# Conformer convolution: taps on VectorE summed in PSUM, 2.5 of 8 channel tiles and the weights' low parts on GpSimd

## The chip, the cores and the metric

One core of one Trainium2 chip runs the whole program. The engines are called PE (TensorE, matmuls; PEld is its weight load), DVE (VectorE), ACT (ScalarE), POOL (GpSimd) and SP (SyncE, which issues the DMAs). The metric is the device time of one execution in microseconds; a lower one is better. "Span" is the time from the first to the last instruction of the profiled execution.

## The reference, cut to what matters

The program is one step of a decoder trunk with two layers, for a prompt of 512 positions and a sample group of 8 sequences with one position each; both share the weights and are handled as 520 columns. Layer 0 has an S5 and an HGRN2 mixer, layer 1 has the Conformer convolution module. Each layer ends with cross-attention into 256 memory tokens and a gated MLP. The part at stake is the mixer of layer 1:

```
z = h @ w_conf_in                      # 1024 -> 2048
a, gate = split(z); u = a * sigmoid(gate)
c[t] = b + sum over 31 taps j of w[j] * ext[t + j]     # per channel, causal; ext = 30 past values, then u
y = silu(layer_norm(c over the 1024 channels)) @ w_conf_out
```

For the prompt the 30 past values are zeros, so tap d (d positions back) touches the columns d to 511 only. For a sample sequence the past values come from a state, and only tap 0 touches the new position.

## The kernel before, in words

Everything is held with channels on the 128 partitions and the 520 columns along the free dimension; 1024 channels are 8 tiles (`KC`). A matmul in full precision is made of three products: activations and weights are each split into a high part of type float32r and a low part (the remainder). `load_w` (L179 to L195) does this for weights: a DMA of 512 KB into `wraw`, a copy by ACT into `whi`, and a subtraction into `wlo` on DVE or, where the caller says so, on POOL, in two halves of 128x512. `mm` (L197) then issues 8 x 3 x 2 = 48 matmuls for one tile of 128 output channels and 520 columns. PSUM tiles come from two pools: `pa` has three buffers of 1024 columns (two banks), `pb` two of 512 (one bank).

The mixer of layer 1 is `mixer1` (L1049 to L1172). `project_first` (L209) computes the first three projection tiles while the norm in front of them is finished. Then, tile by tile, PE makes the gate's and the value's projection (`pcg`, `pca`), and `gate` (L1058) turns them into `u`: DVE multiplies the gate by the norm's factor, ACT takes the sigmoid, DVE multiplies the value by the factor and by the gate.

`conv` (L1069) forms the 31 taps of one tile. ACT writes tap 0 with the bias into `cc`; DVE adds the sample's history `hs`, which `conv_history` (L1454) summed earlier, to the 8 last columns. The other 30 taps go one of three ways:

- DVE: one instruction per tap, c = u * w + c, all in SBUF (L1085). Tiles 1, 3, 6, 7 have 30 such taps, tile 5 has 16.
- POOL: ACT writes u * w into `ct` (three buffers), POOL adds it to `cc` (L1082, L1083). Tiles 0, 2, 4 (`POOL_TAPS`).
- PE: 14 taps of tile 5 (`PE_TAPS`) as matmuls with diagonal matrices (`conv_pe`, L1091), which ACT builds from the identity, and which are summed in a `pb` buffer `pcv`; DVE adds them at the end (L1087).

After the convolution come the keys of layer 1 from the memory tokens (`memory_k`, L1227: 8 tiles, two to a `pb` buffer, evacuated by ACT and DVE as `kf`, `Kh`, `Kl`), four of eight parts of the values (`memory_v`, `pvv`), and the column sums over channels for the LayerNorm (`column_sums`, L228: ones-matmuls over all eight `cc`, into `pcs`). The sums need the finished `cc` of every tile. Then follow the centring (`cmu`), the squares, a second column sum, the scaling, silu, and the output projection.

The order in which each engine takes its instructions is not the written one: the program is built under a planner that simulates the engines' time and places an instruction when its inputs are ready in that simulation (`TileContext(nc, schedule_with_timeline_sim=True)`, L1670). At run time each engine then follows its list in order. `tc.issue_after` pins a few of them, among them the value parts behind the column sums (L1140).

Of the kernel before, what the change touches and what calls it, by code (L numbers as in the profile page):

```python
# [18 lines left out]
P = 128  # L19
# [22 lines left out]
CPAIR = (1, 3)  # L42
CACT = (0, 1, 2, 3, 4, 5, 6, 7)
NE = "VG"
LG = ((0, 0, 0), (0, 0, 0), (0, 1, 1))
POOL_TAPS = {0: 30, 2: 30, 4: 30}
PE_TAPS = {5: 14}
FILL = (4, 6, 5)
# [54 lines left out]
def trunk(ctx, tc, I, O, dbg=None):  # L103
# [47 lines left out]
    def f32(t):  # L151
        return t.bitcast(F32)
# [255 lines left out]

    # ------------------------------------------------------------ S5 and HGRN2 layer
    def mixer0(nxt):  # L410
# [635 lines left out]

    # ------------------------------------------------------------ conformer layer

    def mixer1(bd, nxt, kvp, hs, mem):  # L1049
        nrm, xs = bd.nrm, bd.nrm.xs  # L1050
        l = 1
        with ExitStack() as es:
            cf = es.enter_context(tc.tile_pool(name="cf", bufs=1))
            cw = par[:, PC_CW:PC_CW + CW * KC].rearrange("p (c j) -> p c j", j=CW)

            us, cs = [], []

            def gate(n, pg, pu):  # L1058
                g = slab("cg")
                tt(V, g, pg, r, MUL)  # L1060
                act(g, g, AF.Sigmoid)
                u = slab("cu")
                tt(V, u, pu, r, MUL)
                tt(V, u, u, g, MUL)
                nc.sync.dma_start(O["p_conf"][:, n, :], u[:, LP - (CW - 1):LP])
                nc.sync.dma_start(O["s_conf"][:, n, CW - 2, :], u[:, LP:])
                us.append(u)

            def conv(n):  # L1069
                u = us[n]  # L1070
                c = cf.tile([P, NT], F32, tag="cc", name="cc", bufs=KC)
                cs.append(c)
                if n in CACT:
                    act(c, u, AF.Identity, scale=cw[:, n, CW - 1:CW], bias=pcol(PC_CB, n))
                else:
                    ts(V, c, u, cw[:, n, CW - 1:CW], pcol(PC_CB, n), MUL, ADD)
                tt(V, c[:, LP:], c[:, LP:], hs[:, n, :], ADD)
                for d in range(1, CW - PE_TAPS.get(n, 0)):
                    w = cw[:, n, CW - 1 - d:CW - d]
                    if d > CW - 1 - PE_TAPS.get(n, 0) - POOL_TAPS.get(n, 0):  # L1080
                        t = cf.tile([P, LP], F32, tag="ct", name="ct", bufs=3)
                        act(t[:, d:], u[:, 0:LP - d], AF.Copy, scale=w)  # L1082
                        tt(G, c[:, d:LP], c[:, d:LP], t[:, d:], ADD)  # L1083
                    else:
                        stt(c[:, d:LP], u[:, 0:LP - d], w, c[:, d:LP], MUL, ADD)  # L1085
                if n in part:
                    tt(V, c[:, :LP], c[:, :LP], part[n], ADD)  # L1087

            part = {}

            def conv_pe(n):  # L1091
                nt = PE_TAPS[n]
                u = us[n]
                wh = cf.tile([P, nt], F32R, tag="cwh", name="cwh", bufs=2)
                wl_ = cf.tile([P, nt], F32, tag="cwl", name="cwl", bufs=2)
                act(wh, cw[:, n, :nt], AF.Copy)
                tt(V, wl_, cw[:, n, :nt], f32(wh), SUB)
                uh, ul = (cf.tile([P, CW - 1 + LP], F32R, tag=t, name=t, bufs=1) for t in ("uh", "ul"))
                for t in (uh, ul):
                    G.memset(f32(t[:, :CW - 1]), 0.0)  # L1100
                act(uh[:, CW - 1:], u[:, :LP], AF.Copy)
                tt(V, ul[:, CW - 1:], u[:, :LP], f32(uh[:, CW - 1:]), SUB)
                ps = part[n] = pb("pcv")
                for j0 in range(0, nt, 4):
                    m = min(4, nt - j0)
                    dh = wpool.tile([P, 4, P], F32R, tag="whi", name="dh", bufs=6)
                    dl = wpool.tile([P, 4, P], F32R, tag="wlo", name="dl", bufs=6)
                    for j in range(m):
                        act(dh[:, j], ident, AF.Copy, scale=f32(wh[:, j0 + j:j0 + j + 1]))
                        act(dl[:, j], ident, AF.Copy, scale=wl_[:, j0 + j:j0 + j + 1])  # L1110
                    for j in range(m):
                        o = slice(j0 + j, j0 + j + LP)
                        for i, (a, b) in enumerate(((dh, uh), (dh, ul), (dl, uh))):
                            T.matmul(ps, a[:, j], b[:, o], start=j0 + j == 0 and i == 0,
                                     stop=j0 + j == nt - 1 and i == 2)

            wl = lambda n: load_w(I["w_conf_in"][n])
            p0 = project_first(xs, bd.ws, RC, nrm, CUTC)
            r = nrm.r
            gate(0, *p0[:2])  # L1120
            conv(0)
            for n in range(1, KC):
                pg = p0[2] if n == 1 else mm(pa("pcg"), wl(KC + n), xs)
                pu = mm(pa("pca"), wl(n), xs)
                gate(n, pg, pu)
                if n < 5:
                    conv(n)
            for n in PE_TAPS:
                conv_pe(n)
            for n in range(5, KC):  # L1130
                conv(n)
            kmem = memory_k(1, mem, kvp)
# [40 lines left out]

    # ------------------------------------------------------------ memory keys and values
    mrs = []
# [51 lines left out]
    def memory_k(l, m, kvp):  # L1227
        Kh, Kl = (kvp.tile([P, KC, NM], F32R, tag=t, name=t) for t in ("Kh", "Kl"))
        for n0 in range(0, KC, 2):
            ps = pb("pkk")  # L1230
            for n in (n0, n0 + 1):
                o = ps[:, (n - n0) * NM:(n - n0 + 1) * NM]
                if l == 1:
                    w = raw_w(I["w_xk"][l, n])
                    for k in range(KC):
                        T.matmul(o, w[:, k], m[k], start=k == 0, stop=k == KC - 1)
                else:
                    wh, wl = load_w(I["w_xk"][l, n])
                    for k, (mh, ml) in enumerate(m):
                        for i, (a, b) in enumerate(((wh, mh), (wh, ml), (wl, mh))):  # L1240
                            T.matmul(o, a[k], b, start=k == 0 and i == 0, stop=k == KC - 1 and i == 2)
            kf = slab("kf", n=2 * NM)
            ks = slice(n0, n0 + 2)
            kv = kf.rearrange("p (n m) -> p n m", n=2)
            act(kf, ps, AF.Copy)
            act(Kh[:, ks], kv, AF.Copy)
            tt(V, Kl[:, ks], kv, f32(Kh[:, ks]), SUB)
            nc.sync.dma_start(O["mem_k"][l, :, ks, :], kv)
        return Kh, Kl
# [30 lines left out]

    # ------------------------------------------------------------ cross attention
    def attention(bd, l, kv, ap, nxt, spare=None):
# [169 lines left out]

    # ------------------------------------------------------------ gated MLP with a depthwise convolution
    def conv_history(pool, hs):  # L1454
# [247 lines left out]
```

## Time and profile before

| | before |
|---|---|
| time, median of 3 runs | 1826.97 us (1825.53 to 1831.73) |
| profiled execution: span | 1828.6 us |
| PE, DVE, ACT, POOL busy | 1662.2, 1063.4, 824.8, 718.5 us |
| mean granted clock of TensorE | 0.947 |

The time of the profiled execution is given as its span; what lies around the span is not listed apart. A busy share is a mean over the whole program, in which PE is the busiest engine. Stages differ: in the Conformer convolution, which lies at about 970 to 1220 us of the span, the shares are others, and they are read from windows of the trace.

### The profile page before, as it was taken

How to read it: one execution, taken by the hardware profiler on the slowest of the kernel's cores; microseconds unless marked ns; L12 is line 12 of the kernel's file. 1: busy time of each engine (PE TensorE's matmuls, PEld its weight loads, DVE VectorE, ACT ScalarE, POOL GpSimd, SP SyncE). 2: the span in 40 equal slices, each digit the busy share in tenths (PEclk: the TensorE clock that was granted, in tenths of full speed). 3: DMA queues.
4: the chain of work that ended last, by engine and by line, in shares of the span. 5: the costliest groups of instructions: out<-in, count | busy, mean ns of one | idle time of the engine just before them, and what ended most of it. 6: DMA issues, size and time to landing. Idle time of an engine off the chain costs nothing. (4 is left out here: it accounts for less than half of the span.)

```text
span 1828.6 us, 32823 instructions
## 1 busy us (share of the span) xinstructions
PE 1662.2 (91%) x13050; PEld 1568.3 (86%) x13050; DVE 1063.4 (58%) x1869; ACT 824.8 (45%) x1637; POOL 718.5 (39%) x682
## 2 busy tenths in 40 slices
PE   8987899899898999999999775598989899999996
PEld 8987867898698999999999764388869799999996
DVE  8667486873548423333379998967353842333345
ACT  6424435672456343233356554386245533323343
POOL 2444040511027435252435769514102733525343
PEclk9978799999998999999999887799999999999998
DMA  7332321375631242323222202241672223232331
GB/s 238 101 84 69 108 69 50 119 234 185 233 129 58 87 124 90 104 76 106 80 90 69 61 27 96 74 162 47 196 242 76 70 83 102 82 104 76 110 87 56
DMA packets 81393, 194.76 MB, mean 107 GB/s; under 512 B 21648, under 2 KB 31320, under 8 KB 81240
## 3 DMA queue, kind: packets, MB, share of 16 engines
q1 hardware_dynamic: 81240, 192.66, 33.3%
q8 instruction: 103, 1.69, 0.4%
q14 instruction: 50, 0.41, 0.1%
HBM read 176.67 MB, written 12.47 MB: 103 GB/s over the span
## 5 line engine op out<-in xcount | busy, mean ns | idle before, releaser
L131 ACT ACTIVATE whi<-wraw 128x512 fp32r<-128x512 f32 (+2 forms) x504 | 290.6, 587 | 500.3 <-PE pfo L204 128.0
L138 POOL TENSOR_TENSOR wlo<-wraw,whi 128x512 fp32r<-128x512 f32 x182 | 243.9, 1344 | 319.1 <-ACT whi L131 317.1
L138 DVE TENSOR_TENSOR wlo<-wraw,whi 128x512 fp32r<-128x512 f32 (+2 forms) x322 | 210.2, 664 | 173.7 <-ACT whi L131 163.9
L138 POOL TENSOR_TENSOR cc<-cc,ct 128x509 f32<-128x509 f32 (+15 forms) x90 | 150.5, 1675 | 48.7 <-ACT ct L131 43.0
L141 DVE SCALAR_TENSOR_TENSOR cc<-cu,par,cc 128x511 f32<-128x511 f32 (+25 forms) x136 | 148.1, 1137 | 0.3
L204 PE MATMUL pfb<-xnh,wlo 128*128 128x256 f32 (+1 forms) x672 | 135.8, 283 | 0.0
L204 PE MATMUL pfb<-xnh,whi 128*128 128x256 f32 (+1 forms) x672 | 135.2, 282 | 0.0
L204 PE MATMUL pfb<-xnl,whi 128*128 128x256 f32 (+1 forms) x672 | 135.1, 282 | 0.0
L204 PE MATMUL pfa<-xnh,wlo 128*128 128x256 f32 (+1 forms) x640 | 129.3, 283 | 0.0
L204 PE MATMUL pfa<-xnl,whi 128*128 128x256 f32 (+1 forms) x640 | 128.7, 282 | 0.0
L204 PE MATMUL pfa<-xnh,whi 128*128 128x256 f32 (+1 forms) x640 | 128.6, 282 | 0.0
L204 PE MATMUL pfo<-hlo,whi 128*128 128x256 f32 x604 | 122.0, 282 | 0.0
L204 PE MATMUL pfo<-hhi,wlo 128*128 128x256 f32 x604 | 121.4, 282 | 0.0
L204 PE MATMUL pfo<-hhi,whi 128*128 128x256 f32 x604 | 120.8, 282 | 0.0
L204 PE MATMUL pf<-xnl,whi 128*128 128x256 f32 (+1 forms) x288 | 85.7, 308 | 20.8 <-DVE xnl L141 20.8
L204 PEld LDWEIGHTS pfb<-xnh,whi 128*128 128x128 f32 x672 | 104.2, 188 | 0.0
L204 PEld LDWEIGHTS pfb<-xnh,wlo 128*128 128x128 f32 x672 | 104.2, 189 | 0.0
L204 PEld LDWEIGHTS pfb<-xnl,whi 128*128 128x128 f32 x672 | 104.1, 188 | 0.0
L138 DVE TENSOR_TENSOR fa<-pfa,rstd 128x520 f32<-128x520 f32 x40 | 27.9, 699 | 124.7 <-PE pfa L204 124.7
L204 PEld LDWEIGHTS pfa<-xnh,whi 128*128 128x128 f32 x640 | 99.3, 188 | 0.0
L204 PEld LDWEIGHTS pfa<-xnh,wlo 128*128 128x128 f32 x640 | 99.2, 189 | 0.0
L204 PEld LDWEIGHTS pfa<-xnl,whi 128*128 128x128 f32 x640 | 99.2, 188 | 0.0
(457 smaller groups left out, 4650.9 us busy)
## 6 DMA issues: line engine op xcount, KB each, us to landing
wraw<-w_ffn_in SPq DMA_DIRECT2D x88, 512.0 KB
ck<-cK SPq DMA_DIRECT2D x32, 512.0 KB
cv<-cV SPq DMA_DIRECT2D x32, 512.0 KB
wraw<-w_ffn_out SPq DMA_DIRECT2D x32, 384.0 KB
wraw<-w_ab_in SPq DMA_DIRECT2D x20, 512.0 KB
wraw<-w_ffn_out SPq DMA_DIRECT2D x32, 320.0 KB
wraw<-w_xk SPq DMA_DIRECT2D x16, 512.0 KB
wraw<-w_xv SPq DMA_DIRECT2D x16, 512.0 KB
```

The lines of the kernel that those rows point to most:

```text
L131: A.activation(out, in_, f, **kw)
L138: e.tensor_tensor(out, a, b, op=op)
L141: V.scalar_tensor_tensor(out, in0, s, in1, op0=op0, op1=op1)
L204: T.matmul(ps[:, o:o + m], a[k], b[hv], start=first and k == 0 and i == 0, stop=last and k == n - 1 and i == 2)
```

## The change

1. DVE's taps run in PSUM: ACT writes tap 0 with the bias into a `pb` buffer `pcv`, DVE adds each tap there (u from SBUF, sum from and to PSUM), and the last DVE tap of a tile (d = 1) writes the sum into `cc`. The taps that DVE has are all of tiles 0, 2, 3, 5, 7 and 15 of tile 6.
2. POOL takes tiles 1 and 4 whole and taps 16 to 30 of tile 6 (`POOL_TAPS`); in tile 6 DVE adds its PSUM sum to POOL's sum. The history of the sample is added by POOL, not DVE.
3. The diagonal matmuls (`conv_pe`, `PE_TAPS`) go, with the blocks that ACT built for them.
4. `gate` works in place in PSUM: the gate's product and its sigmoid overwrite `pg`, and the slab `cg` goes.
5. The low parts of the 13 weight tiles that `wl` loads in this stage are made by POOL (`load_w(..., G)`), not DVE.
6. `conv` is a generator. DVE's tiles are one written sequence, of which `CSTEP` = 13 steps are written ahead of each projection tile, and the rest after the last.
7. The keys of layer 1 go to `pa` buffers, four tiles to a buffer.

```diff
@@ -40,11 +40,10 @@
 MEMN = (-1, -1, -1, -1)
 MEMG = ((0, 1, 2, 3), ())
 CPAIR = (1, 3)
-CACT = (0, 1, 2, 3, 4, 5, 6, 7)
 NE = "VG"
 LG = ((0, 0, 0), (0, 0, 0), (0, 1, 1))
-POOL_TAPS = {0: 30, 2: 30, 4: 30}
-PE_TAPS = {5: 14}
+POOL_TAPS = {1: 31, 4: 31, 6: 15}
+CSTEP = 13
 FILL = (4, 6, 5)
 START = (0, (0, 2, 0), 1, (2, 2, 0), (4, 4, 0), 2, (0, 4, 1), (4, 4, 1))
 CVP = (0, 1, 0, 1, 0, 1, 0, 1, 0, 1, 0, 1, 0, 0, 0, 1)
...
@@ -1053,82 +1052,72 @@
             cf = es.enter_context(tc.tile_pool(name="cf", bufs=1))
             cw = par[:, PC_CW:PC_CW + CW * KC].rearrange("p (c j) -> p c j", j=CW)
 
-            us, cs = [], []
+            us, cs = [], [None] * KC
 
             def gate(n, pg, pu):
-                g = slab("cg")
-                tt(V, g, pg, r, MUL)
-                act(g, g, AF.Sigmoid)
+                tt(V, pg, pg, r, MUL)
+                act(pg, pg, AF.Sigmoid)
                 u = slab("cu")
                 tt(V, u, pu, r, MUL)
-                tt(V, u, u, g, MUL)
+                tt(V, u, u, pg, MUL)
                 nc.sync.dma_start(O["p_conf"][:, n, :], u[:, LP - (CW - 1):LP])
                 nc.sync.dma_start(O["s_conf"][:, n, CW - 2, :], u[:, LP:])
                 us.append(u)
 
+            def tap(n, d):
+                return cw[:, n, CW - 1 - d:CW - d]
+
             def conv(n):
-                u = us[n]
-                c = cf.tile([P, NT], F32, tag="cc", name="cc", bufs=KC)
-                cs.append(c)
-                if n in CACT:
-                    act(c, u, AF.Identity, scale=cw[:, n, CW - 1:CW], bias=pcol(PC_CB, n))
-                else:
-                    ts(V, c, u, cw[:, n, CW - 1:CW], pcol(PC_CB, n), MUL, ADD)
-                tt(V, c[:, LP:], c[:, LP:], hs[:, n, :], ADD)
-                for d in range(1, CW - PE_TAPS.get(n, 0)):
-                    w = cw[:, n, CW - 1 - d:CW - d]
-                    if d > CW - 1 - PE_TAPS.get(n, 0) - POOL_TAPS.get(n, 0):
-                        t = cf.tile([P, LP], F32, tag="ct", name="ct", bufs=3)
-                        act(t[:, d:], u[:, 0:LP - d], AF.Copy, scale=w)
-                        tt(G, c[:, d:LP], c[:, d:LP], t[:, d:], ADD)
+                u, np_ = us[n], POOL_TAPS.get(n, 0)
+                c = cs[n] = cf.tile([P, NT], F32, tag="cc", name="cc", bufs=KC)
+                cut = CW - np_
+                act(c[:, LP:], u[:, LP:], AF.Identity, scale=tap(n, 0), bias=pcol(PC_CB, n))
+                tt(G, c[:, LP:], c[:, LP:], hs[:, n, :], ADD)
+                if np_ == CW:
+                    act(c[:, :LP], u[:, :LP], AF.Identity, scale=tap(n, 0), bias=pcol(PC_CB, n))
+                    cut = 0
+                elif np_:
+                    G.memset(c[:, :cut], 0.0)
+                    act(c[:, cut:LP], u[:, :LP - cut], AF.Copy, scale=tap(n, cut))
+                for d in range(cut + 1, CW):
+                    t = cf.tile([P, LP], F32, tag="ct", name="ct", bufs=3)
+                    act(t[:, d:], u[:, 0:LP - d], AF.Copy, scale=tap(n, d))
+                    tt(G, c[:, d:LP], c[:, d:LP], t[:, d:], ADD)
+                if cut:
+                    pc = pb("pcv")
+                    act(pc, u[:, :LP], AF.Identity, scale=tap(n, 0), bias=pcol(PC_CB, n))
+                    yield
+                    for d in range(2, cut):
+                        stt(pc[:, d:], u[:, 0:LP - d], tap(n, d), pc[:, d:], MUL, ADD)
+                        yield
+                    if np_:
+                        stt(pc[:, 1:], u[:, 0:LP - 1], tap(n, 1), pc[:, 1:], MUL, ADD)
+                        tt(V, c[:, :LP], c[:, :LP], pc, ADD)
                     else:
-                        stt(c[:, d:LP], u[:, 0:LP - d], w, c[:, d:LP], MUL, ADD)
-                if n in part:
-                    tt(V, c[:, :LP], c[:, :LP], part[n], ADD)
-
-            part = {}
-
-            def conv_pe(n):
-                nt = PE_TAPS[n]
-                u = us[n]
-                wh = cf.tile([P, nt], F32R, tag="cwh", name="cwh", bufs=2)
-                wl_ = cf.tile([P, nt], F32, tag="cwl", name="cwl", bufs=2)
-                act(wh, cw[:, n, :nt], AF.Copy)
-                tt(V, wl_, cw[:, n, :nt], f32(wh), SUB)
-                uh, ul = (cf.tile([P, CW - 1 + LP], F32R, tag=t, name=t, bufs=1) for t in ("uh", "ul"))
-                for t in (uh, ul):
-                    G.memset(f32(t[:, :CW - 1]), 0.0)
-                act(uh[:, CW - 1:], u[:, :LP], AF.Copy)
-                tt(V, ul[:, CW - 1:], u[:, :LP], f32(uh[:, CW - 1:]), SUB)
-                ps = part[n] = pb("pcv")
-                for j0 in range(0, nt, 4):
-                    m = min(4, nt - j0)
-                    dh = wpool.tile([P, 4, P], F32R, tag="whi", name="dh", bufs=6)
-                    dl = wpool.tile([P, 4, P], F32R, tag="wlo", name="dl", bufs=6)
-                    for j in range(m):
-                        act(dh[:, j], ident, AF.Copy, scale=f32(wh[:, j0 + j:j0 + j + 1]))
-                        act(dl[:, j], ident, AF.Copy, scale=wl_[:, j0 + j:j0 + j + 1])
-                    for j in range(m):
-                        o = slice(j0 + j, j0 + j + LP)
-                        for i, (a, b) in enumerate(((dh, uh), (dh, ul), (dl, uh))):
-                            T.matmul(ps, a[:, j], b[:, o], start=j0 + j == 0 and i == 0,
-                                     stop=j0 + j == nt - 1 and i == 2)
-
-            wl = lambda n: load_w(I["w_conf_in"][n])
+                        stt(c[:, 1:LP], u[:, 0:LP - 1], tap(n, 1), pc[:, 1:], MUL, ADD)
+                        act(c[:, 0:1], pc[:, 0:1], AF.Copy)
+                    yield
+
+            def chain(ns):
+                for n in ns:
+                    yield from conv(n)
+
+            wl = lambda n: load_w(I["w_conf_in"][n], G)
             p0 = project_first(xs, bd.ws, RC, nrm, CUTC)
             r = nrm.r
             gate(0, *p0[:2])
-            conv(0)
+            dve = chain(n for n in range(KC) if POOL_TAPS.get(n, 0) < CW)
             for n in range(1, KC):
+                for _ in range(CSTEP):
+                    next(dve)
                 pg = p0[2] if n == 1 else mm(pa("pcg"), wl(KC + n), xs)
                 pu = mm(pa("pca"), wl(n), xs)
                 gate(n, pg, pu)
-                if n < 5:
-                    conv(n)
-            for n in PE_TAPS:
-                conv_pe(n)
-            for n in range(5, KC):
-                conv(n)
+                if POOL_TAPS.get(n, 0) == CW:
+                    for _ in conv(n):
+                        pass
+            for _ in dve:
+                pass
             kmem = memory_k(1, mem, kvp)
             m = halves(slab("cmu"))
             rp, rs = slab("rstd"), slab("rs")
...
@@ -1226,9 +1215,10 @@
 
     def memory_k(l, m, kvp):
         Kh, Kl = (kvp.tile([P, KC, NM], F32R, tag=t, name=t) for t in ("Kh", "Kl"))
-        for n0 in range(0, KC, 2):
-            ps = pb("pkk")
-            for n in (n0, n0 + 1):
+        step = 4 if l == 1 else 2
+        for n0 in range(0, KC, step):
+            ps = pa("pkk") if l == 1 else pb("pkk")
+            for n in range(n0, n0 + step):
                 o = ps[:, (n - n0) * NM:(n - n0 + 1) * NM]
                 if l == 1:
                     w = raw_w(I["w_xk"][l, n])
...
@@ -1239,13 +1229,15 @@
                     for k, (mh, ml) in enumerate(m):
                         for i, (a, b) in enumerate(((wh, mh), (wh, ml), (wl, mh))):
                             T.matmul(o, a[k], b, start=k == 0 and i == 0, stop=k == KC - 1 and i == 2)
-            kf = slab("kf", n=2 * NM)
-            ks = slice(n0, n0 + 2)
-            kv = kf.rearrange("p (n m) -> p n m", n=2)
-            act(kf, ps, AF.Copy)
-            act(Kh[:, ks], kv, AF.Copy)
-            tt(V, Kl[:, ks], kv, f32(Kh[:, ks]), SUB)
-            nc.sync.dma_start(O["mem_k"][l, :, ks, :], kv)
+                if n % 2 == 0:
+                    continue
+                kf = slab("kf", n=2 * NM)
+                ks = slice(n - 1, n + 1)
+                kv = kf.rearrange("p (n m) -> p n m", n=2)
+                act(kf, ps[:, (n - 1 - n0) * NM:(n + 1 - n0) * NM], AF.Copy)
+                act(Kh[:, ks], kv, AF.Copy)
+                tt(V, Kl[:, ks], kv, f32(Kh[:, ks]), SUB)
+                nc.sync.dma_start(O["mem_k"][l, :, ks, :], kv)
         return Kh, Kl
 
     def memory_v(l, m, kvp, out):
```

Left out are hunks that change comment lines only.

## Rows read from the trace of the kernel before

**Rows 1.** The page: engines' busy time, clock by slice, end of the chain view

```profile
PE 1662.2 (91%) x13050; PEld 1568.3 (86%) x13050; DVE 1063.4 (58%) x1869; ACT 824.8 (45%) x1637; POOL 718.5 (39%) x682
PEclk9978799999998999999999887799999999999998
PE 27%; DVE 2%; DMA 1%; ACT 0%; issue 0%; SPq 0%; DVEq 0%; ACTq 0%
```

**Rows 2.** Windows of the convolution stage: busy us (instructions) of PE, PEld, DVE, ACT, POOL

```profile
972.00:1182.00 210.00, 145.20 (x868) 128.22 (x867) 199.03 (x200) 99.23 (x172) 150.54 (x90) 0.83 0.22 71
1098.00:1111.00 13.00, 0.00 (x0) 0.00 (x0) 12.65 (x20) 0.70 (x1) 12.92 (x2) 0.50 0.12 50
1111.00:1119.00 8.00, 0.86 (x2) 0.78 (x3) 0.00 (x0) 4.92 (x8) 7.69 (x7) 0.50 0.00 2
```

**Rows 3.** Instruction groups of DVE from 972.4 to 1182 us

```profile
L141 DVE SCALAR_TENSOR_TENSOR cc<-cu,par,cc 128x511 f32<-128x511 f32 (+25 forms) x136 | 148.1, 1137 | 0.3
L138 DVE TENSOR_TENSOR wlo<-wraw,whi 128x512 fp32r<-128x512 f32 x24 | 25.8, 1082 | 0.3 <-ACT whi L131 0.3
L138 DVE TENSOR_TENSOR cc<-cc,chs 128x8 f32<-128x8 f32 x8 | 7.5, 939 | 0.0
L138 DVE TENSOR_TENSOR Kl<-kf,Kh 128x512 fp32r<-128x512 f32 x4 | 5.8, 1439 | 8.7 <-ACT Kh L131 8.7
```

**Rows 4.** Instruction groups of POOL from 960 to 1182 us

```profile
L138 POOL TENSOR_TENSOR cc<-cc,ct 128x509 f32<-128x509 f32 (+15 forms) x90 | 150.5, 1675 | 48.7 <-ACT ct L131 43.0
```

**Rows 5.** Timeline (start, length, merged count) of POOL, then DVE, 1111 to 1128 us

```profile
1111.79 2.49 POOL L138 TENSOR_TENSOR cc<-cc,ct 128x486 f32<-128x486 f32 x2
1114.36 1.20 POOL L138 TENSOR_TENSOR cc<-cc,ct 128x484 f32<-128x484 f32 x1
1123.87 3.22 POOL L138 TENSOR_TENSOR cc<-cc,ct 128x507 f32<-128x507 f32 x2
1125.53 3.22 POOL L138 TENSOR_TENSOR cc<-cc,ct 128x506 f32<-128x506 f32 x2
1124.26 3.38 DVE L141 SCALAR_TENSOR_TENSOR cc<-cu,par,cc 128x483 f32<-128x483 f32 x2
1125.90 3.40 DVE L141 SCALAR_TENSOR_TENSOR cc<-cu,par,cc 128x505 f32<-128x505 f32 x2
```

**Rows 6.** Instructions by tile: ns min/median/max, first and last start us

```profile
L138 DVE TENSOR_TENSOR cg<-pcg,rstd x6: 683/686/686, 990.7 to 1081.2; 128x520 f32<-128x520 f32 x6
L138 DVE TENSOR_TENSOR cu<-pca,rstd x7: 685/686/700, 980.0 to 1091.4; 128x520 f32<-128x520 f32 x7
L138 DVE TENSOR_TENSOR cu<-cu,cg x8: 685/687/1443, 976.1 to 1093.9; 128x520 f32<-128x520 f32 x8
```

**Rows 7.** Timeline of DVE at its last taps: first two tiles in turn, then one

```profile
1177.41 1.97 DVE L141 SCALAR_TENSOR_TENSOR cc<-cu,par,cc 128x486 f32<-128x486 f32 x3
1178.05 1.34 DVE L141 SCALAR_TENSOR_TENSOR cc<-cu,par,cc 128x482 f32<-128x482 f32 x2
1178.68 1.46 DVE L141 SCALAR_TENSOR_TENSOR cc<-cu,par,cc 128x485 f32<-128x485 f32 x2
1179.42 1.48 DVE L141 SCALAR_TENSOR_TENSOR cc<-cu,par,cc 128x484 f32<-128x484 f32 x2
```

**Rows 8.** Instruction groups of POOL over the whole span

```profile
L138 POOL TENSOR_TENSOR wlo<-wraw,whi 128x512 fp32r<-128x512 f32 x182 | 243.9, 1344 | 319.1 <-ACT whi L131 317.1 <-PE pfb L204 1.1
L1305 POOL COPY qt<-q 128x8 f32<-128x8 f32 x16 | 5.0, 314 | 65.1 <-DVE q L138 65.1
```

**Rows 9.** Chain view (first row), then timeline of PE: start, length, what

```profile
1283.22 5.75 PE pq L204 x48
1118.14 23.72 PE L1236 MATMUL pkk<-mem,wraw 128*128 128x256 f32 x96 [30.59 <-ACT kf L131]
1141.70 3.60 PE L1265 MATMUL pvv<-wraw,mem 128*128 128x512 f32 x8
1181.71 4.16 PE L232 MATMUL pcs<-cc,cst 128*128 128x256 f32 x10 [1.68 <-DVE cc L141]
```

## The prediction

> **What bounds the kernel now.** I read the page first. TensorE (PE) is busy 91% of the span and its granted clock stands at 9 tenths in most slices; past the first few, the longest dip is in slices 23 to 26, 1006 to 1189 us [rows 1]. The chain of waits covers 27 + 2 + 1 = 30% of the span [rows 1], so it begins near 1280 us and says nothing of the convolution, which lies before that. I therefore went to the windows. From 972 to 1182 us, 210 us long, DVE is busy 199.0 us, POOL 150.5, PE 145.2 at a mean granted clock of 0.83, ACT 99.2 [rows 2]. DVE is the engine without slack. PE waits for it: the column sums of the LayerNorm end only at 1181.7 us, released by a DVE write to `cc` [rows 9]. So the stage is worth what its last tap is worth, and everything behind it (statistics, output projection, attention, MLP) moves with that tap.
>
> What fills DVE is not arithmetic alone. Its 136 taps took 148.1 us, 1137 ns each [rows 3]; undisturbed ones follow each other at 0.635 us when two tiles alternate (1177.41 to 1178.05) and at 0.74 us when one tile's taps follow each other (1178.68 to 1179.42) [rows 7]. POOL's 90 adds took 1675 ns each [rows 4], but 1.285 us while DVE was idle ((1114.36 − 1111.79)/2) [rows 2, 5]. With both busy, each runs at one instruction per 1.65 us (POOL 1123.87 to 1125.53, DVE 1124.26 to 1125.90) [rows 5]: they take turns. From 1098 to 1111 DVE got through 20 instructions and POOL through 2 [rows 2]. Which instructions take part can be read by tile: a product with two SBUF inputs (`cu<-cu,cg`) takes 685 to 1443 ns, while `cg<-pcg,rstd` and `cu<-pca,rstd`, same size, one input in PSUM, took 683 to 700 ns all 13 times, in a stretch where POOL was mostly adding [rows 6]. A tap of before reads `cu` and `cc`, both in SBUF. Undisturbed, 136 taps at 0.635 would be 86 us, so the turns cost DVE about 148 − 86 = 62 us, and its other two-SBUF instructions some more.
>
> **The change part by part.** All counts follow from the loops.
>
> *Taps on DVE.* Tiles 0, 2, 3, 5, 7 have 30 each and tile 6 has 15: 165 instead of 136. Each reads `u` from SBUF and the sum from PSUM, and writes PSUM (the last one of a tile writes `cc`). By rows 6 such a form doesn't take turns with POOL. The trace has no DVE instruction that both reads and writes PSUM. Bounds: 0.635 us (two tiles alternating, as if PSUM were SBUF) and 1.137 us (the mean of before, as if nothing were gained) [rows 3, 7]. Two PSUM buffers would let two tiles alternate, but the code writes one tile after the other, so most taps will follow their own predecessor; I take 0.72 us, near the 0.74 row with some alternation. 165 × 0.72 = 119 us; by the bounds 105 and 188.
>
> *The rest of DVE.* Three gate instructions per tile stay: 24 × 0.69 = 16.6 us [rows 6]. The 24 low parts of weights (25.8 us) and the 8 history adds (7.5 us) leave DVE [rows 3]. The four `Kl` stay (5.8 us at most), one join of tile 6 and two `Vl` come to about 2. In all 24 us. Started at 972: 972 + 24 + 119 = 1115 us.
>
> [...] Writing PSUM no row shows. [...]
>
> *POOL.* Tiles 1 and 4: 30 adds each, tile 6: 14, so 74 instead of 90; at the free pitch 74 × 1.285 = 95 us [rows 5]. New are the low parts of 13 weight tiles, 26 halves × 1.344 = 35 us [rows 8], and 8 history adds of 8 columns, at about 0.31 us (the nearest row is a copy of that size) 2.5 us [rows 8]. Together 133 us. Its adds can start when tile 1's gate runs, about 980 [rows 6], so 1113 us if it never waits; with 1.65 us per add, 1140. The cover for the low parts is that PE has room: after 980 it has 12 projection tiles × 5.75 = 69 us, then keys 8 tiles × 23.72/6 = 32 and four value parts × 3.6 = 14 [rows 9]: 1095 us. If POOL put its adds ahead of the low parts, a pair of projection tiles would cost (8 adds × 1.285 + 4 × 1.344) = 15.7 us, against 11.5 on PE; six pairs are then 25 us later, PE ends at 1120, level with the sum below, and nothing of its room is left.
>
> *ACT.* 74 scaled copies in place of 90 at about 0.7 us, and the 28 diagonal blocks go: less work than before, on an engine with 99.2 us in 210 [rows 2]; beside DVE's taps it costs nothing. A copy for POOL waits for one of three buffers, and behind it in ACT's queue stand the next weights' high parts and the gates; that was so before, when POOL's turns made each of these waits longer.
>
> *Diagonal matmuls.* The 42 that go stood just ahead of the keys, where PE then waited 30.59 us for `kf` [rows 9]: worth nothing. Keys of layer 1 move to the larger PSUM pool, since the small one now holds the sums; four tiles fill one buffer. That shares three buffers with the projection and costs little, as keys follow it. The sigmoid in place in PSUM keeps a buffer longer, through one more DVE product; PE's 20 us to DVE's end cover it.
>
> *Sum.* DVE 1115, POOL 1113, PE 1095. Three engines that end together wait for each other here and there; I add 5 us: 1120. Before it was 1181.7 [rows 9], so 61.7 us earlier. What follows is unchanged and moves along. The profiled execution has a span of 1828.6 us; 1828.6 − 61.7 = 1766.9. The median of the runs shown is 1.6 us under that span (0.1%), so 1765.3; I say 1766.
>
> **The rivals.**
> (a) *The join of tile 6.* DVE adds its PSUM sum to POOL's sum, and POOL's 14 adds for tile 6 are the last in its queue. If that add is queued ahead of tile 7's taps, up to 30 × 0.74 = 22 us of taps stand behind POOL's end at 1113 to 1118, so 1135 to 1140: 1780 to 1785. For it: tile 6 is written before tile 7. Against: the planner puts what is ready first; in rows 7 taps of two tiles alternate.
> (b) *A tap in PSUM is dearer than one in SBUF.* A wait for its own write in PSUM would come on top of 0.74. At 0.90, DVE ends at 972 + 24 + 148 + 5 = 1149: 1795. For it: no row shows a DVE write to PSUM. Against: reading PSUM is free [rows 6]. [...]
> (c) *Slower: PSUM taps still take turns with POOL.* Then 108 POOL instructions each let one tap through per 1.65 us (178 us) and 57 more follow at 0.72 (41 us): 972 + 24 + 178 + 41 = 1215, 33 us later than before: 1860. It decides from a mean tap of (1181.7 − 972 − 24)/165 = 1.126 us on; the mean of before, 1.137, lies just above that, so the change does lose if it removes no turn. Against: 13 of 13 instructions in rows 6. For it: those write SBUF and have no scalar column.
> (d) *Both engines packed without gaps*, 0.65 us a tap by full alternation: POOL's 1113 alone ends the stage: 1758.
>
> **How the numbers follow.** Forecast 0.58 (own range 1759 to 1777), (a) 0.15, (b) 0.14, (c) 0.07, (d) 0.06. 1752 to 1800 holds the forecast, (a), (d) and (b) up to 0.92 us a tap; left out are (c) and the far end of (b). A change under 0.3% (5.5 us) couldn't be told from none: it needs a tap between 1.09 and 1.16 us, 0.01. Faster 0.92, slower 0.07.
>
> **What would show it.** Taps on `pcv` at 0.65 to 0.75 us apart, with no mean above 0.8 while POOL adds; POOL's adds near 1.29 us, not 1.675; DVE and POOL both ending between 1108 and 1125; column sums released near 1120; PE at a higher granted clock from 990 to 1100. The prediction is wrong if taps come 0.85 us apart or more, if DVE stands idle before `cc<-cc,pcv` for over 10 us, or if the last key or value matmul, not a tap, releases the column sums.

## The result, and the profile after

The changed kernel took 1767.23 us (median; 1765.58 to 1769.77) against 1828.51 us for the kernel before on the same chip: a ratio of 0.967, 95% interval 0.9652 to 0.969. The forecast was 1766 us. The profiled execution has a span of 1768.0 us.

The page of the changed kernel, the lines that answer to [rows 1]:

```profile
PE 1646.6 (93%) x13008; PEld 1554.4 (88%) x13008; DVE 995.9 (56%) x1862; ACT 810.9 (46%) x1605; POOL 695.9 (39%) x699
PEclk9979798999999999999999999899999999999998
PE 28%; DVE 2%; DMA 0%; ACT 0%; issue 0%; DVEq 0%; ACTq 0%
```

Of the dip of four slices in the granted clock (slices 23 to 26 in [rows 1]) one slice at 8 tenths is left, the 26th, where the stage ends. DVE is busy 67 us less although it has 29 taps more. Windows of the changed kernel (start:end, length, then busy us and instructions of PE, PEld, DVE, ACT, POOL, granted clock, DMA share, GB/s), to be read against [rows 2]:

```profile
972.00:1122.00 150.00, 130.22 (x847) 116.11 (x846) 135.80 (x203) 87.66 (x148) 127.91 (x109) 0.94 0.32 100
1006.00:1050.00 44.00, 44.00 (x369) 44.00 (x369) 41.22 (x65) 26.59 (x46) 41.20 (x38) 1.00 0.24 75
1100.00:1120.00 20.00, 6.08 (x16) 4.66 (x17) 18.11 (x25) 4.37 (x8) 10.33 (x8) 0.59 0.01 5
```

The window that holds the stage is 150 us long in place of 210. DVE is still the engine with the least slack, but from 1006 to 1050 PE runs without a gap at a clock of 1.00 while DVE and POOL are both over 90% busy. Before, PE had nothing at all from 1098 to 1111 [rows 2]. What is left of PE's wait lies at the end: 6 busy us from 1100 to 1120.

DVE's groups, 960 to 1130 us (line, engine, operation, tiles, count | busy us, mean ns | idle before), which answer to [rows 3]:

```profile
L140 DVE SCALAR_TENSOR_TENSOR pcv<-cu,par,pcv 128x491 f32<-128x491 f32 (+19 forms) x160 | 109.5, 734 | 4.8 <-ACT pcv L130 3.4
...
L137 DVE TENSOR_TENSOR cu<-pca,rstd 128x520 f32<-128x520 f32 x7 | 4.9, 698 | 2.1 <-PE pca L203 2.1
...
L137 DVE TENSOR_TENSOR pcg<-pcg,rstd 128x520 f32<-128x520 f32 x6 | 4.2, 706 | 2.5 <-PE pcg L203 2.5
L137 DVE TENSOR_TENSOR cu<-cu,pcg 128x520 f32<-128x520 f32 x6 | 4.1, 689 | 0.0
L137 DVE TENSOR_TENSOR Kl<-kf,Kh 128x512 fp32r<-128x512 f32 x4 | 4.0, 1012 | 0.0
```

And POOL's in the same stretch, against [rows 4]:

```profile
L137 POOL TENSOR_TENSOR cc<-cc,ct 128x493 f32<-128x493 f32 (+15 forms) x74 | 94.1, 1275 | 4.9 <-ACT ct L130 1.1
L137 POOL TENSOR_TENSOR wlo<-wraw,whi 128x512 fp32r<-128x512 f32 x26 | 33.5, 1299 | 7.7 <-ACT whi L130 7.3 <-ACT cc L130 0.4
...
L137 POOL TENSOR_TENSOR cc<-cc,chs 128x8 f32<-128x8 f32 x8 | 1.6, 200 | 0.7 <-ACT cc L130 0.7
```

A tap costs 734 ns in place of 1137, a POOL add 1275 in place of 1675. Both are close to what they cost undisturbed: 0.70 to 0.74 us a tap [rows 7], 1.20 us an add of 484 columns [rows 5]. The mean alone could hide a few long ones; the view by tile (ns min/median/max) shows that there are none:

```profile
L140 DVE SCALAR_TENSOR_TENSOR pcv<-cu,par,pcv x160: 711/733/754, 980.6 to 1117.7; 128x510 f32<-128x510 f32 x6, 128x509 f32<-128x509 f32 x6, 128x508 f32<-128x508 f32 x6, 128x507 f32<-128x507 f32 x6
```

The two kinds of DVE instruction that still read two SBUF tiles while POOL is adding, `Kl<-kf,Kh` and `Vl<-vf,Vh`, are the ones that are still stretched (means of 1012 and 1286 ns; the shortest of each in the whole program take 676 and 678).

DVE's timeline at the end of the stage (start, length, count):

```profile
1077.91 7.76 DVE L140 SCALAR_TENSOR_TENSOR pcv<-cu,par,pcv 128x490 f32<-128x490 f32 x12
...
1092.87 6.25 DVE L140 SCALAR_TENSOR_TENSOR pcv<-cu,par,pcv 128x510 f32<-128x510 f32 x8 [2.11 <-ACT pcv L130]
...
1102.09 8.47 DVE L140 SCALAR_TENSOR_TENSOR pcv<-cu,par,pcv 128x501 f32<-128x501 f32 x11
1110.97 0.69 DVE L137 TENSOR_TENSOR cc<-cc,pcv 128x512 f32<-128x512 f32 x1 [0.41 <-POOL cc L137]
1111.58 6.83 DVE L140 SCALAR_TENSOR_TENSOR pcv<-cu,par,pcv 128x490 f32<-128x490 f32 x9
1118.45 0.75 DVE L140 SCALAR_TENSOR_TENSOR cc<-cu,par,pcv 128x511 f32<-128x511 f32 x1
```

Read the spacing from a merged row as (length − one tap)/(count − 1). Where two tiles alternate it is (7.76 − 0.73)/11 = 0.64 us; where tile 7 is alone, (8.47 − 0.73)/10 = 0.77. So a tap starts about 0.1 us before the other tile's tap has ended, but 0.04 us after its own predecessor's end. The join of tile 6 waited 0.41 us for POOL. What the end releases is in PE's timeline:

```profile
1082.04 13.90 PE L1257 MATMUL pvv<-wraw,mem 128*128 128x512 f32 x32
1111.72 5.53 PE L231 MATMUL pcs<-cc,cst 128*128 128x256 f32 x14 [15.78 <-DVE cc L137]
1119.45 5.95 PE L231 MATMUL pcs<-cc,cst 128*128 128x256 f32 x18 [2.20 <-ACT cc L130]
```

PE is through with keys and values at 1095.9 and waits 15.8 us; then 14 of the 32 matmuls of the column sums run, and the other 18 once tile 7's last tap (end 1119.2) and the copy of its column 0 by ACT are through.

### The profile page after: what moved, and what is told of

It is laid out like the page before. It is cut to its first block, busy times and chain, and to the rows that moved or that the text cites. A ratio compares the mean times of both kernels' runs of the same rounds, so it can differ in the third digit from the quotient of the medians.

```text
span 1768.0 us, 32710 instructions
## 1 busy us (share of the span) xinstructions
PE 1646.6 (93%) x13008; PEld 1554.4 (88%) x13008; DVE 995.9 (56%) x1862; ACT 810.9 (46%) x1605; POOL 695.9 (39%) x699
## 5 line engine op out<-in xcount | busy, mean ns | idle before, releaser
L137 POOL TENSOR_TENSOR wlo<-wraw,whi 128x512 fp32r<-128x512 f32 x208 | 278.2, 1343 | 324.3 <-ACT whi L130 323.1
L137 DVE TENSOR_TENSOR wlo<-wraw,whi 128x512 fp32r<-128x512 f32 (+2 forms) x296 | 184.4, 634 | 171.8 <-ACT whi L130 163.5
L140 DVE SCALAR_TENSOR_TENSOR pcv<-cu,par,pcv 128x491 f32<-128x491 f32 (+19 forms) x160 | 109.5, 734 | 4.8 <-ACT pcv L130 3.4
L137 POOL TENSOR_TENSOR cc<-cc,ct 128x493 f32<-128x493 f32 (+15 forms) x74 | 94.1, 1275 | 4.9 <-ACT ct L130 1.1
```

The source lines that it names most:

```text
L137: e.tensor_tensor(out, a, b, op=op)
L140: V.scalar_tensor_tensor(out, in0, s, in1, op0=op0, op1=op1)
```

## The experiments

Each ran beside the kernel before on the same chip. "Stage" is read from each profile as the time from DVE's first gate product to the start of `cmu`, ACT's first evacuation of the column sums. In before it is 1182.96 − 972.42 = 210.5 us, from these rows of DVE and ACT:

```profile
972.42 0.70 DVE L138 TENSOR_TENSOR cg<-pf,rstd 128x520 f32<-128x520 f32 x1
1182.96 0.38 ACT L131 ACTIVATE cmu<-pcs 128x256 f32<-128x256 f32 x1 [18.87 <-PE pcs L232]
```

| kernel | median us (range) | ratio, 95% interval | stage us |
|---|---|---|---|
| changed | 1767.23 (1765.58 to 1769.77) | 0.9671, 0.9652 to 0.969 | 144.4 |
| 1 only sums in PSUM | 1773.07 (1770.54 to 1773.18) | 0.9705, 0.9688 to 0.9721 | 157.0 |
| 2 sums in SBUF | 1841.03 (1840.78 to 1846.58) | 1.0087, 1.0066 to 1.0108 | 220.4 |
| 3 low parts on DVE | 1781.57 (1779.24 to 1784.27) | 0.9755, 0.9735 to 0.9775 | 158.7 |
| 4 tile 6 last | 1765.23 (1761.39 to 1766.65) | 0.9667, 0.9649 to 0.9686 | 142.0 |
| 5 taps in one line | 1781.35 (1778.32 to 1782.79) | 0.9735, 0.9718 to 0.9751 | 159.0 |
| 6 gate in SBUF | 1769.08 (1767.98 to 1773.48) | 0.9677, 0.9662 to 0.9691 | 149.4 |
| 7 column sums elsewhere | 1766.46 (1762.88 to 1767.98) | 0.9655, 0.9641 to 0.9669 | 144.6 |
| 8 both 4 and 7 | 1761.08 (1757.55 to 1762.17) | 0.9625, 0.9611 to 0.9639 | 140.3 |
| 9 PSUM sums and low parts | 1778.36 (1775.17 to 1781.9) | 0.9737, 0.9719 to 0.9754 | 158.9 |
| 10 changed, again | 1764.43 (1763.77 to 1767.07) | 0.9663, 0.9649 to 0.9677 | 144.3 |
| 11 both, again | 1760.68 (1757.05 to 1764.0) | 0.9637, 0.962 to 0.9655 | 140.3 |

The stage column repeats to 0.1 us where the same program ran twice, while the moment at which it starts does not: 976.14 us in the changed kernel, 970.12 in its repeat, 967.78 in kernel 1. So a difference of 3 us between two medians says little, and one between two stage lengths says more.

**1. Only the sums move to PSUM.** The kernel before with its own split of the taps, its diagonal matmuls and its low parts on DVE; the diagonal matmuls' buffer gets a name of its own, and the keys use the larger buffers as in the change.

```diff
+                pc = pb("pcv")
+                act(pc, u[:, :LP], AF.Identity, scale=cw[:, n, CW - 1:CW], bias=pcol(PC_CB, n))
+                for d in range(2, CW - PE_TAPS.get(n, 0)):
+                    stt(pc[:, d:], u[:, 0:LP - d], cw[:, n, CW - 1 - d:CW - d], pc[:, d:], MUL, ADD)
+                stt(c[:, 1:LP], u[:, 0:LP - 1], cw[:, n, CW - 2:CW - 1], pc[:, 1:], MUL, ADD)
+                act(c[:, 0:1], pc[:, 0:1], AF.Copy)
...
-                ps = part[n] = pb("pcv")
+                ps = part[n] = pb("ppe")
```

> The kernel before, with one thing changed: DVE's taps (tiles 1, 3, 6, 7 and 16 of tile 5) are summed in PSUM. POOL keeps tiles 0, 2, 4, PE its 14 diagonal taps, DVE the weights' low parts; the keys use the larger PSUM buffers, since the small ones now hold sums. Theory (the turns between DVE's two-SBUF taps and POOL's adds were the loss): 136 taps x 0.66 = 90 us, gates 17, low parts 26, history 7, keys and join 7: DVE ends at 972 + 147 = 1119, POOL's 90 adds near 1110; 1766 to 1773 us, nearly the whole gain. Rival (the gain comes from moving work: fewer adds on POOL, low parts off DVE, no diagonal matmuls): less than half the gain, over 1797 us, with adds still above 1.5 us.

Measured: 1773.07 us, at the upper edge of the theory's range: 54 of the 61 us. DVE's groups in this kernel:

```profile
L141 DVE SCALAR_TENSOR_TENSOR pcv<-cu,par,pcv 128x507 f32<-128x507 f32 (+24 forms) x131 | 90.7, 732 | 1.8 <-ACT pcv L131 0.7
L138 DVE TENSOR_TENSOR wlo<-wraw,whi 128x512 fp32r<-128x512 f32 x26 | 25.5, 989 | 2.4 <-ACT whi L131 2.4
L138 DVE TENSOR_TENSOR cu<-cu,cg 128x520 f32<-128x520 f32 x8 | 8.2, 1030 | 0.0
```

The taps are at 732 ns with the split of the work unchanged. The low parts and the gate's product, which still read two SBUF tiles, stay at 989 and 1030 ns. By the stage, the place of the sum is worth 210.5 − 157.0 = 53.5 of 66.1 us, and the work that the change moves the other 12.6. By the medians that work is worth only 6 to 9 us; the stage of this run's profile began 2.3 us earlier than that of the changed kernel's repeat and 8.4 us earlier than that of its first profile. The keys' move to the larger buffers is in this run too; experiment 2 keeps it and gains nothing, so it isn't what made the difference.

**2. The changed kernel with its sums in SBUF.** One line; everything else as changed.

```diff
-                    pc = pb("pcv")
+                    pc = cf.tile([P, LP], F32, tag="pcv", name="pcv", bufs=2)
```

> The changed kernel with one thing undone: the tap sums of DVE lie in an SBUF tile of the same name instead of a PSUM buffer; split of tiles, low parts on POOL, gates and written order as changed. Theory: 108 POOL instructions let one tap through per 1.65 us (178 us) and 57 taps follow at 0.7 (40 us): DVE ends near 1215, 1850 to 1870 us, slower than the kernel before. Rival (moved work is what counts): under 1800 us.

Measured: 1841.03 us, 0.7 to 1.1% slower than the kernel before, though below the theory's range. The slowdown that rival (c) feared of PSUM sums is what the same kernel shows with SBUF sums. Groups of DVE and then of POOL, 960 to 1200 us:

```profile
L140 DVE SCALAR_TENSOR_TENSOR pcv<-cu,par,pcv 128x491 f32<-128x491 f32 (+25 forms) x160 | 187.5, 1215 | 3.6 <-ACT pcv L130 2.2
```

```profile
L137 POOL TENSOR_TENSOR cc<-cc,ct 128x493 f32<-128x493 f32 (+15 forms) x74 | 117.3, 1589 | 21.3 <-ACT cc L130 11.2 <-ACT ct L130 6.5
```

Its timeline near the end, DVE's rows and then POOL's:

```profile
1155.80 15.40 DVE L140 SCALAR_TENSOR_TENSOR pcv<-cu,par,pcv 128x510 f32<-128x510 f32 x10 [0.88 <-ACT pcv L130]
...
1175.94 7.64 DVE L140 SCALAR_TENSOR_TENSOR pcv<-cu,par,pcv 128x499 f32<-128x499 f32 x10
```

```profile
1156.51 18.96 POOL L137 TENSOR_TENSOR cc<-cc,ct 128x493 f32<-128x493 f32 x12 [11.21 <-ACT cc L130]
```

Ten taps take 15.4 us beside POOL's twelve adds, and ten take 7.6 us once POOL is done. The gates still run in PSUM here and stay at 0.68 to 0.69 us; only the form with two SBUF inputs pays. The time came out under what the theory gave: it let every POOL instruction meet a tap, but POOL stood idle 11.2 us before the last of its stretches, and the mean tap was 1.215 us.

**3. The low parts back on DVE.**

```diff
-            wl = lambda n: load_w(I["w_conf_in"][n], G)
+            wl = lambda n: load_w(I["w_conf_in"][n])
```

> The changed kernel with one thing undone: the low parts of the 13 weight tiles are made by DVE again. Theory (DVE sets the end, POOL 8 us behind it): 26 x 0.61 to 1.08 us = 16 to 28 us more on DVE, POOL ends 30 us earlier: 1781 to 1795 us. Rival (POOL sets the end, through the join and through the weights that PE waits for): no slower than 1768 us.

Measured: 1781.57 us, inside the theory's range, 14 us above the changed kernel. Groups of DVE, 960 to 1140 us, and POOL's last adds in the timeline:

```profile
L140 DVE SCALAR_TENSOR_TENSOR pcv<-cu,par,pcv 128x508 f32<-128x508 f32 (+28 forms) x160 | 109.4, 732 | 3.8 <-ACT pcv L130 2.7
L137 DVE TENSOR_TENSOR wlo<-wraw,whi 128x512 fp32r<-128x512 f32 x26 | 22.4, 871 | 3.5 <-ACT whi L130 3.4
```

```profile
1070.50 19.84 POOL L137 TENSOR_TENSOR cc<-cc,ct 128x495 f32<-128x495 f32 x15 [1.09 <-ACT ct L130]
```

POOL is through at 1090.3 and DVE at 1127.7. The low parts take 22 us on DVE, and the stage is 14 us longer. From the first gate product to the end of the last tap DVE is busy 150.1 us in place of 132.6 and idle 7.0 in place of 10.4: part of the new work filled idle time, and two of the 26 lie ahead of the stage. DVE then sets the end alone.

**9. The PSUM sums with the old split, and the low parts on POOL.** Experiment 1 and the opposite of the line in experiment 3.

> The kernel of the run with PSUM sums alone (old split: POOL tiles 0, 2, 4, PE 14 diagonal taps, DVE 136 taps), and in addition the low parts of the 13 weight tiles made by POOL. Theory (with turns gone, the busier of two engines ends the stage): POOL has 90 x 1.25 + 26 x 1.29 = 146 us in a row, DVE 26 us less than in that run; POOL ends the stage 152 to 157 us after its start: 1773 to 1779 us, so the move alone brings nothing and needs the new split of tiles. Rival (DVE's low parts were what counted): DVE ends it, 1747 to 1755 us.

Measured: 1778.36 us, no better than without the move (1773.07; their intervals overlap by a hair). POOL's groups and its last row in the timeline:

```profile
L138 POOL TENSOR_TENSOR cc<-cc,ct 128x509 f32<-128x509 f32 (+15 forms) x90 | 116.1, 1291 | 7.9 <-ACT ct L131 3.1
L138 POOL TENSOR_TENSOR wlo<-wraw,whi 128x512 fp32r<-128x512 f32 x26 | 35.6, 1375 | 3.9 <-ACT whi L131 3.9
```

```profile
1080.00 51.16 POOL L138 TENSOR_TENSOR cc<-cc,ct 128x489 f32<-128x489 f32 x38
```

POOL now ends at 1131.2, with DVE's last tap long done (1114.2). So beside the sums in PSUM the move of the low parts and the rest of the change (the new split with what goes with it) are worth something only together: the low parts alone overload POOL (0.9737), the rest with the low parts on DVE overloads DVE (0.9755), neither is 0.9705, both are 0.967.

**5. Taps in written order.** The taps are pinned behind each other, so two tiles can't alternate.

```diff
+            def tapped(*args):
+                with tc.issue_after(prev[-1]) if prev else ExitStack():
+                    i = V.scalar_tensor_tensor(*args, op0=MUL, op1=ADD)
...
-                        stt(pc[:, d:], u[:, 0:LP - d], tap(n, d), pc[:, d:], MUL, ADD)
+                        tapped(pc[:, d:], u[:, 0:LP - d], tap(n, d), pc[:, d:])
```

> The changed kernel with each DVE tap tied behind the tap written before it, so that no two tiles alternate; nothing else changes. Theory (a tap behind its own predecessor takes 0.775 us in PSUM, one in alternation 0.64; the planner's alternation is why the taps cost 110 us and not the 119 that I predicted): 135 taps x 0.135 = 18 us more on DVE, less some of its 5 us of idle time: 1780 to 1786 us. Rival (a tap costs the same either way, the pitch at the end came from POOL's adds): 1765 to 1769 us.

Measured: 1781.35 us, as the theory had it. DVE's timeline:

```profile
1108.63 0.68 DVE L137 TENSOR_TENSOR cc<-cc,pcv 128x512 f32<-128x512 f32 x1
1109.23 20.05 DVE L1105 SCALAR_TENSOR_TENSOR pcv<-cu,par,pcv 128x507 f32<-128x507 f32 x26
```

(20.05 − 0.75)/25 = 0.772 us from tap to tap; the duration itself is hardly changed (median 739 ns against 733). The planner's alternation of two tiles is worth 14.6 us of stage. The pin also puts the join of tile 6 ahead of 27 of tile 7's taps, but POOL was in time for it, so this is not where the time went.

**4. Tile 6 last.** So that its join is not ahead of tile 7's taps, and two tiles alternate to the end.

```diff
-            dve = chain(n for n in range(KC) if POOL_TAPS.get(n, 0) < CW)
+            dve = chain((0, 2, 3, 5, 7, 6))
```

> The changed kernel with DVE's tiles written in the order 0, 2, 3, 5, 7, 6 instead of 0, 2, 3, 5, 6, 7. In the changed kernel tile 6 held one of the two PSUM sums until POOL was through with it, so tile 7 began late (2.1 us idle) and ran its 30 taps alone at 0.775 us. Theory: tile 7 now alternates with its neighbours at 0.64 us: 30 x 0.135 = 4 us and the 2 us of idle time go, down to POOL's end at 1111 and the join: 1761 to 1764 us. Rival (POOL's end and the join are already the bound): 1766 to 1769 us.

Measured: 1765.23 us, between the two ranges; neither is borne out. DVE's last write to `cc` did come early, at 1108.74, 137.8 us after the first gate product in place of 143.1. PE's timeline shows where most of the gain went:

```profile
1106.76 9.76 PE L231 MATMUL pcs<-cc,cst 128*128 128x256 f32 x32 [16.01 <-ACT cc L130]
```

All 32 matmuls of the column sums stand in one block that starts only at 1106.76: the sums for six finished tiles, which could have run in the 16 us that PE waited, did not. Their target `pcs` comes from the same two `pb` buffers that hold the tap sums of the last two tiles; that this held them back is what the next two kernels test. DVE then waits 4.68 us for `cmu`.

**7 and 8. The column sums in the larger buffers, alone and with tile 6 last.** Column 0 of `cc` is also written ahead of the taps, not copied after them; in 8 the tiles are written as in 4, and the sums take them in the order in which they end (the last line below; 7 keeps the old list).

```diff
-                        act(c[:, 0:1], pc[:, 0:1], AF.Copy)
...
+                        act(c[:, 0:1], u[:, 0:1], AF.Identity, scale=tap(n, 0), bias=pcol(PC_CB, n))
...
-                ps = column_sums([halves(c)[hv] for c in cs], hv, last)
+                ps = column_sums([halves(cs[n])[hv] for n in (0, 1, 2, 3, 4, 5, 7, 6)], hv, last, pa)
```

> The changed kernel with the first column sums in the larger PSUM buffers and column 0 of a tile copied before its taps, not after. In the changed kernel no column sum could start before tile 6's join at 1111.7, since both small buffers held tap sums, and the sums waited 2.2 us for ACT's copy of column 0 behind the last tap. Theory: seven tiles' sums are done when the last tap ends, and 2 to 3 us go: 1763 to 1766 us. Rival (the sums end with the last tap plus the same chain): 1767 us.

> Tile 6 written last, as in the run before with that name, and the column sums in the larger buffers with tile 6 last in them. With tile 6 last alone, DVE's last tap came 10 us earlier, but all 32 column sums then ran behind it, 16 us after PE's last matmul, and took until 1113. Theory: both gains add: stage 5 us shorter on DVE and the sums 4 us shorter: 1758 to 1762 us. Rival (POOL's end near 1107 and PE's idle clock bind): 1764 to 1767 us.

Measured: 1766.46 us for 7, between its two ranges and not to be told from the changed kernel (its stage is 144.6 us), and 1761.08 us for 8, inside the theory's range. PE's timeline in 8:

```profile
1093.51 2.36 PE L231 MATMUL pcs<-cc,cst 128*128 128x256 f32 x10
1106.64 2.10 PE L231 MATMUL pcs<-cc,cst 128*128 128x256 f32 x4 [10.77 <-DVE cc L140]
1109.65 2.10 PE L231 MATMUL pcs<-cc,cst 128*128 128x256 f32 x4 [0.91 <-DVE cc L137]
```

The sums of six tiles are done by 1095.9, and only four matmuls stand behind the last write to `cc` (`cc<-cc,pcv` ends at 1109.60). In 7 the same pieces run early, but tile 7's taps still come one by one at the end (0.76 us from start to start). The place of the sums pays once the taps no longer set the end: neither edit alone gives much, both give 4 us of stage. The stage as defined stops at the first half of the columns, though, and in 7 and 8 the second half's sums follow at once (0.9 us later, 4.9 in the changed kernel). Up to DVE's first scaling product (`cc<-cc,rstd`) the gains are 2.6 us for 4, 1.0 for 7 and 5.2 for both. The larger buffers and the early column 0 were not tried apart.

**10 and 11. The changed kernel and kernel 8 again, on one chip.** No new edit.

> The changed kernel itself, beside the next one on the same chip. Theory: 0.965 to 0.969 of the kernel before.

> The kernel with tile 6 last and the column sums in the larger buffers once more, on the same chip as the changed kernel. Theory: 4 to 8 us below it, 0.961 to 0.964 of the kernel before. Rival (the difference of the earlier runs was one of chips): within 2 us of it.

Measured: 1764.43 and 1760.68 us, 3.75 us apart, just under the 4 to 8 that were expected and above the rival's 2. The sign is the same as between the earlier runs, the stage lengths repeat (144.3 and 140.3 us), and the intervals of the two ratios overlap slightly (0.9649 to 0.9677, 0.962 to 0.9655). Kernel 8 has the lowest median in both rounds; its lead, 0.2 to 0.5% by medians or ratios, is small.

**6. The gate through SBUF.** Part 4 of the change undone.

```diff
-                tt(V, pg, pg, r, MUL)
-                act(pg, pg, AF.Sigmoid)
+                g = slab("cg")
+                tt(V, g, pg, r, MUL)
+                act(g, g, AF.Sigmoid)
...
-                tt(V, u, u, pg, MUL)
+                tt(V, u, u, g, MUL)
```

> The changed kernel with the gate's product and sigmoid in an SBUF slab again, so that the last product of the gate has two SBUF inputs. Theory (such a product takes turns with POOL): 8 x up to 0.76 us = up to 6 us more: 1769 to 1774 us. Rival (its place in DVE's list is hidden by waits for PE): 1765 to 1769 us.

Measured: 1769.08 us, within the spread of the changed kernel. The stage is 5 us longer in its profile, though, and one instruction stands out. DVE's timeline, and POOL's over the same microseconds:

```profile
1002.07 1.37 DVE L140 SCALAR_TENSOR_TENSOR pcv<-cu,par,pcv 128x504 f32<-128x504 f32 x2
1003.35 7.70 DVE L137 TENSOR_TENSOR cu<-cu,cg 128x520 f32<-128x520 f32 x1
1010.96 2.64 DVE L140 SCALAR_TENSOR_TENSOR pcv<-cu,par,pcv 128x503 f32<-128x503 f32 x4
```

```profile
1003.05 1.29 POOL L137 TENSOR_TENSOR wlo<-wraw,whi 128x512 fp32r<-128x512 f32 x1
...
1009.23 1.25 POOL L137 TENSOR_TENSOR cc<-cc,ct 128x501 f32<-128x501 f32 x1
1015.48 1.30 POOL L137 TENSOR_TENSOR wlo<-wraw,whi 128x512 fp32r<-128x512 f32 x1 [5.00 <-PE pcg L203]
```

One product of two SBUF tiles held DVE for 7.7 us, to 1011.05, while POOL worked without a gap up to 1010.48; POOL then waited 5.0 us for PE. Whether the time itself pays for it, these runs can't tell.

## Why the prediction was right

**The mechanism.** The step that carried it, that a tap with its sum in PSUM doesn't take turns with POOL, held for all 160 such taps (711 to 754 ns). Experiments 1 and 2 show it from both sides: that step alone gives 54 us, and without it the rest of the change loses 14. In these runs the median tap took 733 ns with one SBUF input and its output in PSUM (changed kernel), and 1130 ns with two SBUF inputs and its output in SBUF (experiment 2).

The 62 us that the prediction put on the turns are some 8 too many: it set durations (1137 ns) against a distance from start to start (0.635 us, where taps overlap); the durations of the 136 taps fell from 148.1 to 94.4 us in experiment 1. The prediction also calls 1181.7 the end of the column sums; that row is the start of their last block [rows 9], and the sum uses it rightly, as the end of the last tap.

**The size of the terms.**

- *Taps, 165 × 0.72 = 119 us: too large by 10.* From the first tap (980.63) to the end of the last (1119.2) are 138.6 us. Less 21 us of other instructions and 8.6 us of waits (the groups above, the join, and 2.6 us for two `Vl`) 109 remain, 0.66 us a tap. This is the term that was mis-sized. "One tile after the other" with "some alternation" underrated the planner: it alternated two tiles for nearly all taps but the first sixteen of tile 0 (0.77 to 0.79 apart) and the thirty of tile 7 (0.77). That is above the 0.74 of rows 7, but PSUM isn't the reason: in experiment 2 the same taps, with the sum in SBUF and POOL done, come at (7.64 − 0.73)/9 = 0.77 as well.
- *Friction, 5 us: too small by 5.* After the first tap DVE waited 3.6 us ahead of taps, mostly for ACT to fill `pcv` (the prediction had put ACT at nothing), 4.6 us for PE's projections and 0.4 us for POOL at the join; 1.9 us more lie before it.
- *The rest of DVE, 24 us*: 21 after the first tap and 2.6 before it.
- *POOL, to 1113*: to 1110.9. Its adds took 94.1 us (95), the low parts 33.5 (35), the history 1.6 (2.5).
- *PE, keys and values through at 1095*: at 1095.9. The cover for moving the low parts to POOL was there.
- *The start, 972*: 976.14 in this execution, 970.12 in the repeat of the same program. Of the stage itself, 147.6 us were forecast up to the last tap and 143.1 came; a late start nearly made up for it. So the profiled end of 1119.2 is 976.1 + 23.8 + 108.8 + 10.5 (start, rest, taps, waits), where the forecast had 972 + 24 + 119 + 5 = 1120. The taps 10 us too dear were offset by friction and start, 5 and 4 us too small. That the mechanism held is earned; that the end came out within 1 us is luck.

**A tap with its sum in PSUM and in SBUF.** Where two tiles alternate, taps of 486 to 488 columns took 722 to 724 ns on average with the sum in PSUM (changed kernel, while POOL adds) and 707 to 709 with it in SBUF (the kernel before, 1168 to 1182 us, POOL done); from start to start that is 0.64 us and 0.635 [rows 7]. So the place of the sum mattered little to an undisturbed tap. The order mattered more: 0.77 us behind the own predecessor stands against 0.64 in alternation, and experiment 5 makes a stage of 159.0 us in place of 144.4 of it. What holds a tap back behind its own predecessor was not tested apart from the order.

**The rivals.** (a) came in its order but not at its price: the join stood ahead of ten of tile 7's taps, but DVE waited only 0.41 us there for POOL, as the twenty taps ahead had kept it busy until then. (b) is refuted by the durations and by the distances, 0.64 and 0.77 us; the latter is a little outside the 0.65 to 0.75 that the prediction named as its sign. (c) did not come; with the sums in SBUF, experiment 2 measured 1841, under the 1860 worked out, as not every POOL instruction met a tap. (d), both packed, is not reached; kernel 8 comes to about 3 us from its 1758.

## What to carry to other kernels

When two engines are both far over their undisturbed instruction times, look by tile at which forms are stretched and which are not: moving one operand of the stretched form out of SBUF was worth 54 us here, and rebalancing the work between the engines 6 to 13 more, and only when the low parts and the tiles were moved together. Give chained accumulations on DVE a second, independent chain to alternate with (0.64 us a tap against 0.77, 14.6 us of stage in experiment 5), and see to it that the buffers which hold long sums are not the ones that the next stage's first matmuls need (with tile 6 last, 4 us of stage in kernel 8).

## What was not expected of the hardware

The turns between DVE and POOL were not always even. In the kernel before, POOL got through 2 adds while DVE got through 20 instructions [rows 2, second window]; in experiment 6 a product on DVE stood 7.7 us while POOL went through six instructions without a gap (1003.05 to 1010.48). In other stretches they alternated at 1.65 us [rows 5]. Both lockouts met an engine whose instructions followed each other without a pause (DVE alternating two tiles, POOL alternating low parts and adds); that this is the condition was not tested. A mean over a group can therefore hide one long instruction, as in experiment 6 (eight gate products, median 866 ns, longest 7697), and the maximum in the view by tile is the place to see it.
